# A gated block of mLSTM and differential attention: the queue between mLSTM and branch B, a bank at the start, two loads and two stores

## The chip, the cores and the metric

The kernel runs on one core of one Trainium2 chip. The metric is the device time of one execution in microseconds, smaller being better. The kernel before took 1668.07 us (median of three runs, 1665.59 to 1670.39).

Names of engines: PE is TensorE (matmuls; PEld its weight loads), DVE is VectorE, ACT is ScalarE, POOL is GpSimd, SP is SyncE, which here does nothing but issue DMAs. ACT issues some DMAs too.

## The reference

One layer over a sequence of 1024 rows of width 1024, batch 1, all in fp32:

```python
h = rmsnorm(x, norm_g)
a_q, a_k, a_v, a_o, a_z, a_g, b_q, b_k, b_v, b_z, g_a, g_b = split(h @ w_in)
qk = silu(centred_depthwise_conv(concat(a_q, a_k), ml_conv_w))
hm = rmsnorm(mlstm(mq, mk, mv, forward gates) + mlstm(flipped, backward gates), ml_norm_g)   # 4 heads of 256
y_a = hm * sigmoid(a_o) * silu(a_z)
att = softmax(q0 k0) v - lam * softmax(q1 k1) v        # 8 heads, rope on q and k
y_b = rmsnorm(att, da_subln_g) * (1 - lambda_init) * silu(b_z)
mix = sigmoid(g_a + gb[0]) * (y_a @ w_branch_a) + sigmoid(g_b + gb[1]) * (y_b @ w_branch_b)
out = rmsnorm(x + mix @ w_out, final_g)
```

## The kernel before

**Arithmetic.** Every large product is made of three matmuls: each fp32 operand is split into a rounded high part H and a remainder L, and HH, HL and LH are summed in a PSUM bank. So a weight block of 128 columns is loaded into a tile `raw` (L194, 512 KB), rounded into `wH` by ACT (L231) and its remainder `wL` formed by POOL (L237 in eight pieces or L239 in one). There are two `raw` tiles and three each of `wH` and `wL`.

**Stages, in order of time.** (1) The opening: x is normalised (`norm_a` to `norm_c`, in four steps of ACT, DVE and POOL for each of eight row tiles), transposed on PE into banks `xps[0..7]`, and split into `hH`/`hL`. `xps[6]` is a bank of the pool `pj`, which has two; the others are `T` banks. The first projections (`g0`, `g1`, `g2`) start while the second half of x is still being normalised, each in a `pj` bank. `first_part` (L697) has ACT read each of the eight `xps` once more. (2) The other projections for mLSTM, by a seven-product scheme. (3) Attention, its results `yb` stored to DRAM. (4) mLSTM, four heads in four chunks of 256 rows, woven with units of the gate projections `ga`/`gb` (bank `pj`; their tanh goes through the tile `gt` to DRAM). Its results `ya` are stored by `out` (L1401), two per half head. (5) Branch B: eight tiles of `yb` are loaded (`load_y`, L1486, four buffers `yraw`), split into `sl_yb` by ACT (L1488) and DVE (L1489), and multiplied with eight blocks of `w_branch_b`; the first three blocks go through `first_units` (L1506), which interleaves them over the contraction index k, so that it can begin with one `yb` tile. The five others are `mix_units`. (6) Branch A and the output product.

**What sets the order.** `build` makes one list of units, and `run` (L549) emits them, loading a weight block ahead by a rule (`ahead`): the blocks that the next unit needs, and beyond those one more where `room` allows. Within `keep(...)` the engines named keep the order of emission; the others are ordered by the framework's scheduler. Before the change, `keep` held PE alone from the end of the opening on, so SP's queue was the scheduler's. SP issues in order: an issue whose wait is not met holds all behind it.

The places the change touches: the test `ahead` (L552), `first_part` (L695), the store in `out` (L1401), the start of `ml_units` (L1419), where `x["k"](3)` loads the tile `akf` of chunk 3 (L1213) and `x["gb"](0)` the tile `gb` (L1222, gate values read 128 times over), two lines of the opening (L1731), and the lines of `build` between mLSTM and branch B (L1790 on). `weigh` (L1250, L1251) scales the transposed `akf` into `kwH`, `kwL`, which the `state` products (L148) read; `scores` builds its mask with POOL from `gb` (L1305) and ACT (L1307).

## Time and profile before

| | us |
|---|---|
| median of three runs | 1668.07 |
| lowest, highest | 1665.59, 1670.39 |
| the profiled execution | 1669.31 |
| its span | 1667.0 |
| mean granted TensorE clock in it | 0.996 |

The span runs from the first to the last instruction; 2.3 us of the execution lie around it. A row of the timeline is: start, duration, engine, line, operation, output<-input, size, count, and in brackets the engine's idle time just before, with what is thought to have ended it. A row of the windows is: the stretch, its length, then for PE, PEld, DVE, ACT and POOL the busy time and the number of instructions, then the granted PE clock (1.00 is full), the DMA engines' busy share and GB/s. A row of the waits is: the engine that waited, its tile and line, what ended the wait, total us, times, longest.

### The profile page before, as it was taken

How to read it: one execution, taken by the hardware profiler on the slowest of the kernel's cores; microseconds unless marked ns; L12 is line 12 of the kernel's file. 1: busy time of each engine (PE TensorE's matmuls, PEld its weight loads, DVE VectorE, ACT ScalarE, POOL GpSimd, SP SyncE). 2: the span in 40 equal slices, each digit the busy share in tenths (PEclk: the TensorE clock that was granted, in tenths of full speed). 3: DMA queues.
4: the chain of work that ended last, by engine and by line, in shares of the span. 5: the costliest groups of instructions: out<-in, count | busy, mean ns of one | idle time of the engine just before them, and what ended most of it. 6: DMA issues, size and time to landing. Idle time of an engine off the chain costs nothing. (4 is left out here: it accounts for less than half of the span.)

```text
span 1667.0 us, 25342 instructions
## 1 busy us (share of the span) xinstructions
PE 1629.7 (98%) x9335; PEld 1373.8 (82%) x9335; DVE 1018.8 (61%) x1829; ACT 769.3 (46%) x1547; POOL 654.5 (39%) x707
## 2 busy tenths in 40 slices
PE   7999999999999999999999999999999999999998
PEld 5898778878779888889878888888988987888887
DVE  5733787686754776876777676604666664244533
ACT  6433555555533554544554455524566654132221
POOL 3744676767653552533435253032222221222000
PEclk9999999999999999999999999999999999999999
DMA  5433444344452322213232222139876437452222
GB/s 181 152 126 129 123 134 140 117 136 126 127 151 64 89 58 71 63 40 90 57 82 54 62 58 64 44 95 304 254 222 195 151 108 259 153 167 90 76 99 79
DMA packets 189710, 199.76 MB, mean 120 GB/s; under 512 B 11929, under 2 KB 143346, under 8 KB 189586
## 3 DMA queue, kind: packets, MB, share of 16 engines
q1 hardware_dynamic: 187378, 194.19, 38.5%
q10 hardware_dynamic: 2208, 3.95, 0.6%
q8 instruction: 74, 1.21, 0.3%
q14 instruction: 50, 0.41, 0.1%
HBM read 124.60 MB, written 56.72 MB: 109 GB/s over the span
## 5 line engine op out<-in xcount | busy, mean ns | idle before, releaser
L579 PE MATMUL pj<-hH,wH 128*128 128x512 f32 x640 | 261.9, 409 | 1.8 <-POOL rsy L666 1.0
L579 PE MATMUL pj<-hH,wL 128*128 128x512 f32 x640 | 251.5, 393 | 0.8 <-POOL wL L237 0.8
L579 PE MATMUL pj<-hL,wH 128*128 128x512 f32 x640 | 250.7, 392 | 0.6 <-DVE hL L735 0.6
L1101 DVE TENSOR_REDUCE nm<-S 128x1 f32<-128x1024 f32 x128 | 150.7, 1219 | 109.2 <-PE S L1098 109.2
L239 POOL TENSOR_TENSOR wL<-raw,wH 128x1024 fp32r<-128x1024 f32 x33 | 82.4, 2499 | 175.7 <-ACT wH L231 173.3
L1103 ACT ACTIVATE e<-S,nm 128x1024 f32<-128x1024 f32 x128 | 142.7, 1130 | 7.0 <-DVE nm L1101 7.0
L579 PEld LDWEIGHTS pj<-hH,wL 128*128 128x128 f32 x640 | 120.3, 188 | 28.2 <-POOL wL L237 2.2
L579 PEld LDWEIGHTS pj<-hH,wH 128*128 128x128 f32 x640 | 121.0, 189 | 21.5 <-POOL rsy L666 1.4
L579 PEld LDWEIGHTS pj<-hL,wH 128*128 128x128 f32 x640 | 120.8, 189 | 20.3 <-DVE hL L735 1.4
L1122 ACT CAST pH<-T 128x512 fp32r<-128x512 f32 x128 | 68.9, 589 | 147.7 <-PE T L152 147.7
L1098 PE MATMUL S<-kst,qq 64*128 64x512 f32 x768 | 106.2, 408 | 0.0
L231 ACT CAST wH<-raw 128x1024 fp32r<-128x1024 f32 x47 | 49.4, 1052 | 99.3 <-PE pj L579 70.0
L1109 DVE SCALAR_TENSOR_TENSOR e<-e,r,e 128x1024 f32<-128x1024 f32 x64 | 94.0, 1469 | 1.8
L1098 PEld LDWEIGHTS S<-kst,qq 64*128 64x128 f32 x768 | 67.3, 184 | 29.2 <-issue 9.4
L579 PE MATMUL pj<-sl_yb,wH 128*128 128x512 f32 x288 | 88.6, 389 | 0.0
L376 PE MATMUL T<-TH,wH 128*128 128x512 f32 x256 | 85.8, 394 | 2.3 <-ACT u L383 2.3
L523 DVE SCALAR_TENSOR_TENSOR pj<-cin,cols,pj 128x512 f32<-128x512 f32 x128 | 86.9, 746 | 0.0
L376 PE MATMUL T<-TH,wL 128*128 128x512 f32 x256 | 85.3, 394 | 1.6 <-ACT u L383 1.5
L1123 DVE TENSOR_TENSOR pL<-T,pH 128x512 fp32r<-128x512 f32 x128 | 82.0, 680 | 5.9 <-ACT pH L1122 5.9
L217 POOL TENSOR_TENSOR wL<-raw,wH 128x512 fp32r<-128x512 f32 x32 | 47.0, 1486 | 77.7 <-ACT wH L216 72.3
L152 PEld LDWEIGHTS T<-ident,e 128*128 128x128 f32 x512 | 54.9, 141 | 23.8 <-issue 23.7
L601 PE MATMUL pj<-wH,hH 128*128 128x256 f32 x256 | 74.3, 290 | 0.0
(409 smaller groups left out, 4464.4 us busy)
## 6 DMA issues: line engine op xcount, KB each, us to landing
raw<-in_w_in_dram SPq DMA_DIRECT2D x84, 512.0 KB, 3.9
kst<-hl SPq DMA_DIRECT2D x64, 128.0 KB, 2.4
qq<-hl SPq DMA_DIRECT2D x64, 128.0 KB, 2.4
x<-in_x_dram SPq DMA_DIRECT2D x8, 512.0 KB, 5.3
avH<-tz SPq DMA_DIRECT2D x16, 256.0 KB, 2.0
cak<-y SPq DMA_DIRECT2D x16, 256.0 KB, 2.7
cakH<-cin SPq DMA_DIRECT2D x16, 256.0 KB, 4.6
cakL<-tz SPq DMA_DIRECT2D x16, 256.0 KB, 4.4
```

The costliest lines, as they stand in the source:

```text
L152: self.t.transpose(out, in_, self.ident[0:k, 0:k])
L239: self.p.tensor_tensor(out=wL, in0=raw, in1=wHf, op=ALU.subtract)
L376: self.t.matmul(ps, lhsT=l[:, k, :], rhs=r[:, k, :], start=(first and k == 0 and m == 0), stop=(k == 3 and m == 2), skip_group_check=not f ...
L523: v.scalar_tensor_tensor(out=acc, in0=raw[:, o + x:o + x + 512], scalar=w(x), in1=acc, op0=ALU.mult, op1=ALU.add)
L579: self.t.matmul(ps, lhsT=l[:, k, :], rhs=r, start=(n == 0), stop=(n == 23))
L601: self.t.matmul(ps[:, i, :], lhsT=l, rhs=r[:, k, :], start=(kh == 0 and k == 0 and m == 0), stop=(kh == 1 and k == 3 and m == 2))
L1098: self.t.matmul(ps[:, o], lhsT=qq[r, x, c], rhs=k[r, y, o], start=(m == 0), stop=(m == 2))
L1101: v.tensor_reduce(out=nm, in_=ps, axis=AX.X, op=ALU.max, negate=True)
L1103: a.activation(out=e, in_=ps, func=AF.Exp, bias=nm[:, 0:1], accum_out=Z[:, j, t:t + 1])
L1109: v.scalar_tensor_tensor(out=e0, in0=e, scalar=r[:, 0:1], in1=e0, op0=ALU.mult, op1=ALU.add)
L1122: a.copy(pH[:, :, s], ps)
L1123: v.tensor_tensor(out=pL[:, :, s], in0=ps, in1=pH[:, :, s].bitcast(F32), op=ALU.subtract)
```

## The change

Five edits.

1. From the end of mLSTM to the end of branch B's first group SP keeps the order of emission (`keep(E.PE, E.SP)` ... `keep(E.PE)`), and while `hold` is set no weight block is loaded before its unit asks. `wb(1)` and `wb(2)` are called by hand behind the first four and in front of the second four loads of `yb`.
2. The last two stores of `ya` (last head, second half) are issued by ACT instead of SP.
3. At the start of mLSTM the load of `gb` chunk 0 is issued ahead of that of `akf` chunk 3.
4. In the opening, ACT's second reading of `xps[6]`, the `pj` bank, is done where that of `xps[1]` was, and the latter with the rest.
5. `first_part` makes its tile when it is first needed (as `fp(6)` now comes before `fp(2)`).

```diff
@@ run
-                ahead = lambda k: nxt < need or nxt <= need + (4 if k[0] == "sw" else 1) and room(k)
+                ahead = lambda k: nxt < need or not self.hold and nxt <= need + (4 if k[0] == "sw" else 1) and room(k)
@@ first_part
-        if i == 0:
+        if k not in self.f:
@@ out
-            q.dma_start(out=self.ya[2 * n + i][:, half * 512:(half + 1) * 512], in_=g)
+            (a if n == NH_A - 1 and half == 1 else q).dma_start(out=self.ya[2 * n + i][:, half * 512:(half + 1) * 512], in_=g)
@@ ml_units
-        un += x["k"](3) + x["gb"](0) + x["v"](3) + x["k"](2) + x["v"](2) + x["k"](1) + x["v"](1) + x["HL"](0)
+        un += x["gb"](0) + x["k"](3) + x["v"](3) + x["k"](2) + x["v"](2) + x["k"](1) + x["v"](1) + x["HL"](0)
@@ build, opening
-            w.add(ld(0), sp(0), fp(0), sp(1), g0[0], do(self.transpose_last), *[sp(i) for i in range(2, 8)], ld(1), fp(1), nA(4), nA(5), *g0[1:k])
-            w.add(nB(4), nC(4), nA(6), ld(2), nB(5), nC(5), nA(7), fp(2, 3, 4, 5, 6, 7), nB(6), nC(6), nB(7), nC(7), *g1[:k])
+            w.add(ld(0), sp(0), fp(0), sp(1), g0[0], do(self.transpose_last), *[sp(i) for i in range(2, 8)], ld(1), fp(6), nA(4), nA(5), *g0[1:k])
+            w.add(nB(4), nC(4), nA(6), ld(2), nB(5), nC(5), nA(7), fp(1, 2, 3, 4, 5, 7), nB(6), nC(6), nB(7), nC(7), *g1[:k])
@@ build, mLSTM to branch B
-            w.add(wb(0), *rest[:3])
+            w.add(keep(E.PE, E.SP), do(lambda: setattr(self, "hold", True)), wb(0), *rest[:3])
...
-            w.add(*loads[:4], wb(1), *rest[5:12], *loads[4:], *rest[12:])
+            w.add(*loads[:4], wb(1), *rest[5:12], wb(2), *loads[4:], *rest[12:], do(lambda: setattr(self, "hold", False)))
...
-            w.add(leave("h"), enter("wr", "wr"), *group)
+            w.add(leave("h"), enter("wr", "wr"), *group, keep(E.PE))
```

The order of PE and of DVE is the same in both kernels. What moves is on SP and ACT, and one row of POOL changes its form.

SP at the end of mLSTM, before. `ya6`/`ya7` with `gA_14793`/`gA_14795` are the first halves of the last head, with `gA_14971`/`gA_14973` the second; `raw_15094` and `raw_15240` are the blocks 2 and 3 of `w_branch_b`; `yb0` to `yb3` are the first four tiles of attention's result.

```order
L194 DMA raw_15094<-in_w_branch_b_dram 128x8x128
L1401 DMA ya6_88<-gA_14793 128x512
L1401 DMA ya7_89<-gA_14795 128x512
L194 DMA raw_15240<-in_w_branch_b_dram 128x8x128
L1401 DMA ya6_88<-gA_14971 128x512
L1401 DMA ya7_89<-gA_14973 128x512
L1486 DMA yraw_15138<-yb0_90 128x1024
L1486 DMA yraw_15144<-yb1_91 128x1024
L1486 DMA yraw_15150<-yb2_92 128x1024
L1486 DMA yraw_15156<-yb3_93 128x1024
```

The same place now (`raw_15183` is block 2; blocks 3 and 4 follow behind `yb7`):

```order
L1401 DMA ya6_88<-gA_14793 128x512
L1401 DMA ya7_89<-gA_14795 128x512
L1486 DMA yraw_15128<-yb0_90 128x1024
L1486 DMA yraw_15134<-yb1_91 128x1024
L1486 DMA yraw_15140<-yb2_92 128x1024
L1486 DMA yraw_15146<-yb3_93 128x1024
L194 DMA raw_15183<-in_w_branch_b_dram 128x8x128
L1486 DMA yraw_15187<-yb4_94 128x1024
```

Two weight loads and two stores no longer stand ahead of the four loads of `yb`.

ACT at the same place, now. `gt_15165` and `gt_15223` are the tanh of the last two gate banks, `sl_yb_15130` the first high part that branch B multiplies, `wH_15181` the high part of block 2.

```order
L994 DMA tga6_72<-gt_15080 128x512
L1401 DMA ya6_88<-gA_14971 128x512
L1401 DMA ya7_89<-gA_14973 128x512
L993 ACTIVATE gt_15165<-pj_15086,gbh_213 128x512
L994 DMA tga7_73<-gt_15165 128x512
L1488 CAST sl_yb_15130<-yraw_15128 128x1024
L1488 CAST sl_yb_15136<-yraw_15134 128x1024
L993 ACTIVATE gt_15223<-pj_15168,gbh_213 128x512
L1488 CAST sl_yb_15142<-yraw_15140 128x1024
L994 DMA tga7_73<-gt_15223 128x512
L1488 CAST sl_yb_15148<-yraw_15146 128x1024
L231 CAST wH_15181<-raw_15183 128x1024
```

Before, the cast of block 2 stood between the first two `sl_yb`; it now stands behind the fourth, and the two stores stand ahead of `gt_15165`.

The opening on ACT, and the start of mLSTM on SP, as pieces of the difference. On ACT `T` and `pj` are the banks `xps`, `x_226` and `x_228` the fifth and sixth row tiles:

```order
 L734 ACTIVATE hH_187<-T,g_in 128x512
-L697 ACTIVATE f<-T,g_in 128x512
+L697 ACTIVATE f<-pj,g_in 128x512
 L664 ACTIVATE sq,ssqx<-x_226 128x1024
 L664 ACTIVATE sq,ssqx<-x_228 128x1024
```

ACT's second reading of the `pj` bank moves ahead of the squares of the later row tiles, and a `T` bank takes its old place among the readings behind them. On SP `cak_106` is the key tile of the first head and `gg` the gate rows:

```order
 L1169 DMA yb_97<-zg 128x512 x2
+L1222 DMA gb<-gg 128x2x256
 L1213 DMA akf<-cak_106 128x512
-L1222 DMA gb<-gg 128x2x256
 L1230 DMA vH<-avH_3_129 128x2x256
```

The load of `gb` and that of `akf` have changed places; the rest of the queue stands as it was.

## Prediction

> **What bounds it now.** First the page's busy times, then the waits of the engine with the largest, then the timeline round its longest ones.

> ```profile
> PE 1629.7 (98%) x9335; PEld 1373.8 (82%) x9335; DVE 1018.8 (61%) x1829; ACT 769.3 (46%) x1547; POOL 654.5 (39%) x707
> ```

> PE works in 98 % of a span of 1667.0 us. It does the same matmuls in the same order in both kernels, so all that the change can move is PE's idle time, 1667.0 - 1629.7 = 37.3 us, and the stretches in which PE runs at less than the full clock. The waits of PE name two that lie at places of the change; the other two come below, as rows of the timeline.

> ```profile
> PE T L1506 <- ACT sl_yb L1488: 2.7, 1, 2.7
> PE T L148 <- issue: 1.4, 1, 1.4
> ```

> The windows show the clock there and in two undisturbed stretches.

> ```profile
> 1394.60:1401.00 6.40, 5.94 (x13) 4.36 (x14) 5.73 (x4) 5.05 (x6) 2.42 (x1) 0.50 0.86 296
> 1403.00:1430.88 27.88, 27.88 (x124) 23.09 (x123) 11.68 (x12) 9.47 (x9) 4.28 (x2) 1.00 0.74 270
> 1131.00:1135.00 4.00, 3.99 (x16) 3.58 (x17) 1.31 (x3) 0.73 (x2) 0.00 (x0) 0.57 1.06 397
> 1210.00:1212.00 2.00, 1.47 (x11) 1.26 (x11) 1.00 (x3) 2.00 (x7) 0.00 (x0) 1.00 0.68 244
> ```

> Behind the wait of 2.7 us the granted clock was 0.50 for 6.4 us, and behind that of 1.4 us it was 0.57 over 4 us. Where PE idled 2.00 - 1.47 = 0.53 us in pieces, at 1210, it stayed 1.00. So I read a gap of 1.4 us and more as costing twice: itself, and a stretch at half clock behind it.

> **Edits 1 and 2, the boundary.** SP's queue, then the three instructions it and PE wait for, then PE:

> ```profile
> 1367.05 0.99 SPq L1401 DMA_DIRECT2D ya<-gA  x2
> 1385.35 0.38 SPq L194 DMA_DIRECT2D raw<-in_w_branch_b_dram  x1
> 1385.83 1.01 SPq L1401 DMA_DIRECT2D ya<-gA  x2
> 1386.93 9.22 SPq L1486 DMA_DIRECT2D yraw<-yb  x5
> ```

> ```profile
> 1381.93 3.40 POOL L237 TENSOR_TENSOR wL<-raw,wH 128x128 fp32r<-128x128 f32 x8 [3.61 <-ACT wH L231]
> 1382.67 1.41 DVE L1400 SCALAR_TENSOR_TENSOR gA<-T,mlg,gA 128x512 f32<-128x512 f32 x2 [3.56 <-PE T L152]
> 1393.50 1.04 ACT L1488 CAST sl_yb<-yraw 128x1024 fp32r<-128x1024 f32 x1 [6.28 <-DMA tga<-gt]
> ```

> ```profile
> 1391.54 0.39 PE L579 MATMUL pj<-hH,wL 128*128 128x512 f32 x1
> 1394.60 0.80 PE L1506 MATMUL T<-sl_yb,wH 128*128 128x512 f32 x1 [2.67 <-ACT sl_yb L1488]
> 1395.85 0.79 PE L1506 MATMUL T<-sl_yb,wH 128*128 128x512 f32 x1 [0.46 <-DVE sl_yb L1489]
> 1430.88 0.62 PE L579 MATMUL pj<-sl_yb,wH 128*128 128x512 f32 x2
> ```

> SP issues in order and stood still from 1368 to 1385.35, because the third weight block reuses a `raw` tile which POOL reads until 1381.93 + 3.40 = 1385.33. Behind it come two stores of `ya`, whose data DVE has ready at 1382.67 + 1.41 = 1384.08, and only then `yb0`, at 1386.93. ACT's cast starts 6.6 us later; the row names a DMA of `tga`, but its input `yraw` was on the way since 1386.93, and PE starts 0.06 us behind the cast's end at 1394.54.

> Clean cadence: 27.88 us / 123 weight loads = 0.2267 us a matmul. The 1391.54 matmul lets the next start at 1391.77. The three blocks of the first group are 3 x 8 x 2 x 3 = 144 matmuls, 144 x 0.2267 = 32.64 us, so without a wait the next group would start at 1424.41 and not at 1430.88. That is **6.47 us**: 2.83 of gap and 3.64 of the 0.46 wait and the half clock (6.40 x 0.50 = 3.2).

> Does all of it go? Now `yb0` to `yb3` stand right behind the two stores of 1367.05, so at about 1368; `yb3` and all behind it may start some us later, if a DMA semaphore is still in use by a `tga` store. Durations, from the tile view of the `yb` loads, from the issue of `tga6` at 1374.69, and from three rows at the boundary:

> ```profile
> DMA to landing us min/median/max: 4.4/5.7/7.6
> tga<-gt ACTq DMA_DIRECT2D x1, 256.0 KB, 2.0
> ```

> ```profile
> 1386.53 0.69 ACT L993 ACTIVATE gt<-pj,gbh 128x512 f32<-128x512 f32 x1 [4.14 <-PE pj L579]
> 1394.58 1.23 DVE L1489 TENSOR_TENSOR sl_yb<-yraw,sl_yb 128x1024 fp32r<-128x1024 f32 x1 [10.49 <-ACT sl_yb L1488]
> 1395.62 2.42 POOL L239 TENSOR_TENSOR wL<-raw,wH 128x1024 fp32r<-128x1024 f32 x1 [10.29 <-ACT wH L231]
> ```

> The worst start is 1374.69 + 2.0 = 1376.7, the worst landing 1376.7 + 7.6 = 1384.3. The first cast then waits not for data but for its turn on ACT, behind `gt_15165` (end 1387.22) and its store: 1387.6 to 1388.6, the second to 1389.7; DVE's parts end at 1389.8 and 1391.0. All are ready before 1391.77. **What is late next** is block 2, whose cast now stands behind the fourth `sl_yb`: `gt_15223` waits for the last gate matmul (1391.9), with the two casts and a store it ends near 1395.4, block 2's cast near 1396.4, POOL's part 2.42 later near 1398.9. PE multiplies two blocks with the first tiles before it asks for block 2, at its 37th matmul, 1391.77 + 36 x 0.2267 = 1399.9: about 1 us of margin for H and 1.5 for L. The two stores on ACT occupy it about 1 us (SP's pair took 1.01) between `gt` activations with 4.14 us of idle: nothing. The stores of 1367.05 stay. Bounds of the step: 0 (`yb` still held), and -6.5; below that nothing is idle. I take **-6.5**.

> [...]

> **Edits 4 and 5, the opening.**

> ```profile
> 19.91 0.74 ACT L697 ACTIVATE f<-T,g_in 128x512 f32<-128x512 f32 x1
> 19.93 0.74 DVE L735 SCALAR_TENSOR_TENSOR hL<-pj,g_in,hH 128x512 fp32r<-128x512 f32 x1
> 22.56 0.64 ACT L1002 COPY gt<-pj 128x512 f32<-128x512 f32 x1
> 23.34 0.47 PE L579 MATMUL pj<-hH,wH 128*128 128x512 f32 x1 [1.01 <-POOL rsy L666]
> 28.96 0.70 ACT L697 ACTIVATE f<-pj,g_in 128x512 f32<-128x512 f32 x1
> 29.71 0.50 PE L579 MATMUL pj<-hH,wH 128*128 128x512 f32 x1 [0.65 <-ACT f L697]
> 29.96 0.81 DVE L677 TENSOR_SCALAR x<-x,rsy,rsv 128x1024 f32<-128x1024 f32 x1
> 32.57 1.91 PE L152 MATMUL T<-ident,x 128*128 128x128 f32 x16
> 34.23 0.48 PE L579 MATMUL pj<-hH,wH 128*128 128x512 f32 x1
> ```

> Two groups of matmuls wait for a `pj` bank: at 23.34 for the one that ACT's copy frees at 23.20 (the row names POOL, which frees no bank), and at 29.71 for `xps[6]`, which ACT reads only at 28.96 to 29.66. Read early, it is free at about 21.4, and both waits go: 1.01 + 0.65 = 1.66. But the early reading shares the bank with DVE's row at 19.93 and cannot start before 20.67, 0.76 later than the reading that stood there. What follows on ACT slips by as much, the squares and norms of x among it, so that the last row tile, ready at 29.96 + 0.81 = 30.77, comes at about 31.55. PE now arrives at the transposes at 32.57 - 1.66 = 30.91 and takes 1.66 for sixteen; those of the last tile cannot begin before 31.55. If all wait, they end at 33.21 (gain 1.02); if only the last half, at 32.57 (1.66). I take **-1.2**, nearer the first, with bounds 0 (the slip goes further down the norms) and -1.66.

> **Edit 3, the start of mLSTM.**

> ```profile
> 1117.77 0.42 SPq L1213 DMA_DIRECT2D akf<-cak  x1
> 1118.25 0.45 SPq L1222 DMA_DIRECT2D gb<-gg  x1
> ```

> ```profile
> 1125.91 0.60 PE L152 MATMUL T<-ident,akf 128*128 128x128 f32 x4
> 1126.58 1.25 POOL L1305 TENSOR_SCALAR_AFFINE_SELECT W<-gb 128x128 f32<-128x128 f32 x4 [2.92 <-DMA gb<-gg]
> 1126.90 1.56 ACT L1307 ACTIVATE W<-W,gc_negM 128x128 f32<-128x128 f32 x4 [6.14 <-POOL W L1305]
> 1128.37 0.66 ACT L993 ACTIVATE gA<-pj,gbh 128x512 f32<-128x512 f32 x1
> 1130.01 0.36 PE L148 MATMUL T<-vH,kwH 128*128 128x258 f32 x1 [1.41 <-issue]
> ```

> The gap of 1.41 us at 1130.01 is the end of a chain in ACT's order: `gb` lands at 1126.55, POOL and ACT make the mask until 1128.46, ACT's `gA` and a store follow, then `kwH`, which PE needs. With `gb` ahead, its issue is 1118.25 - 1117.77 = 0.48 earlier and its packets no longer queue behind `akf`'s 256 KB, some 0.65 us at the 397 GB/s of the window above: 1.1 earlier, so the gap becomes 0.3. `akf` pays: it lands by as much later than now, and PE asks for it at 1125.91, which may cost 0.2 to 0.6 there. I take **-1.0** for the gap (bounds +0.6, if `akf` is later than that and the chain gains nothing, and -1.4). The half clock behind it cost at most 4.00 x (1 - 0.57) = 1.72; some of the products there wait for `kwH` and `kwL` anyway, so I take **-1.5** (bounds 0 and -1.72). Queue behind it: everything else on SP stands where it stood.

> **Sum.** 1669.31 - 6.5 - 1.2 - 1.0 - 1.5 = **1659.1** for the profiled execution, which was 1.2 above the median of the runs, 1668.07; the median would give 1657.9. I say 1659.0.

> **Rivals.**
> - *The gap at 1130 or its half clock stays* (`akf` late, or 0.3 to 0.5 us being enough): without -1.5 the sum is 1660.6, without -1.0 too 1661.6. For it: one row of 0.57 is little to know the clock by. Against: 1.00 at 1210. Chance 0.30.
> - *Another wait takes the boundary's place*: block 2, or a `yb` tile, late by a few us. It costs up to the 3.64 of the half clock and as much again in waiting: 1661 to 1667. For it: about 1 us of margin; against: the landing times leave the tiles 10 us. Chance 0.08.
> - *The change doesn't bring the loads forward* (`yb` still held to 1385 by a semaphore of a store): only opening and mLSTM remain, 1669.31 - 3.7 = 1665.6. Against: those stores land in 2.0 us. Chance 0.04.
> - *The slow stretches do not come from the gaps* and stay: 2.83 + 0.46 + 1.2 + 1.0 = 5.5 is left, 1663.8. [...] Against: both stretches begin right behind the two longest waits in question. Chance 0.05.
> - *The half clock moves to another cluster of short waits*, since PE reaches them in another rhythm; PE's other waits of this kind are around 1 us. It costs 3: 1662. Chance 0.04.
> - *Slower than before*: block 2's load is now held in SP's order behind `yb3`. If `yb3`'s wait puts block 2's remainder D us late, PE stalls by D - 1.5 and pays the 3.2 of half clock again. That eats the gain of 10.2 from D = 1.5 + 10.2 - 3.2 = 8.5 us on, and at D = 14 the time is 1674.8. For it: the block is no longer loaded ahead by rule. Against: its cast would have to come at 1405, with `yb3` expected to land 20 us before that. Chance 0.04.

> **How the numbers follow.** The forecast with all terms, 1659.1, has 0.45; the rivals 0.30, 0.08, 0.04, 0.05, 0.04, 0.04. The runs of the kernel before spread over 4.8 us, so 2.4 either way on top. The least sum by the bounds is 1669.31 - 6.5 - 1.66 - 1.4 - 1.72 = 1658.0, less 2.4 and the 1.2 by which the profiled execution lay above the median: 1654. Above, the first rival's 1661.6 plus 2.4 is 1664, and 1665 takes in the clock rival and part of the boundary's: what is left out is about 0.15. About 0.3 %, 5.0 us, is what a measurement of this kernel can tell from no change: faster is below 1663.1. The forecast, the first rival, half of the second and half of the fifth make 0.81; same has the rest of these, the third, the fourth and a little of the last, 0.16; slower 0.03.

> **What the profile of the changed kernel would show.** Right: `yraw` issued at about 1368 behind the first `ya` stores; `sl_yb` cast behind `gt_15165`; no gap at L1506's first matmul, and 1.00 in the 6 us behind it; about 32.6 us from it to the next group; no waits for a `pj` bank at 23.3 and 29.7; at L148 a gap below 0.5 us with clock 1.00 behind it. Wrong: a wait of L1506 for `wH` or `wL` of block 2 some 8 us into the group; a wait of the `akf` transposes near 1125; a window of 0.5 in any place where before it was 1.00; a wait for `x` at the transposes longer than the 0.65 taken here.

## The result, and the profile after

The changed kernel took 1658.62 us (median of four runs, 1657.96 to 1659.14), the kernel before 1667.24 us beside it (1665.59 to 1670.39). The ratio is 0.9946 with a 95% interval of 0.9929 to 0.9963: faster by 8.6 us. The profiled execution took 1657.96 us with a span of 1656.1 us, against 1669.31 and 1667.0. The ratios below leave out one execution, of 4640 us, of the kernel with edit 2 alone.

The page's busy times after, and two rows of PE's waits:

```profile
PE 1624.8 (98%) x9335; PEld 1371.3 (83%) x9335; DVE 1019.7 (62%) x1829; ACT 769.0 (46%) x1547; POOL 654.0 (39%) x700
...
PE T L152 <- DVE x L677: 1.4, 3, 0.8
...
PE T L152 <- DMA akf<-cak: 0.2, 1, 0.2
```

PE's idle time fell from 37.3 to 31.3 us, and its busy time by 4.9 us though it does the same 9335 matmuls: that is the clock, as the rows of windows below show. The lines of L1506, of L148 with "issue" and of the two `pj` banks are gone; two small waits came in their place, 0.76 us of that for `x` and the 0.2 for `akf`.

The boundary after, from the timelines of SP, ACT, DVE, POOL and PE:

```profile
1362.57 0.98 SPq L1401 DMA_DIRECT2D ya<-gA  x2
1363.64 8.91 SPq L1486 DMA_DIRECT2D yraw<-yb  x4
1379.98 0.38 SPq L194 DMA_DIRECT2D raw<-in_w_branch_b_dram  x1
...
1383.15 2.00 ACT L1488 CAST sl_yb<-yraw 128x1024 fp32r<-128x1024 f32 x2 [0.40 <-ACT gt L993]
1389.98 1.05 ACT L231 CAST wH<-raw 128x1024 fp32r<-128x1024 f32 x1
...
1384.23 2.36 DVE L1489 TENSOR_TENSOR sl_yb<-yraw,sl_yb 128x1024 fp32r<-128x1024 f32 x2 [4.62 <-ACT sl_yb L1488]
...
1391.16 2.63 POOL L239 TENSOR_TENSOR wL<-raw,wH 128x1024 fp32r<-128x1024 f32 x1 [11.30 <-ACT wH L231]
...
1387.07 0.39 PE L579 MATMUL pj<-hH,wL 128*128 128x512 f32 x1
1387.30 0.62 PE L1506 MATMUL T<-sl_yb,wH 128*128 128x512 f32 x2
1419.94 0.62 PE L579 MATMUL pj<-sl_yb,wH 128*128 128x512 f32 x2
```

The loads of `yb` stand right behind the first stores of `ya`; the first cast waits for `gt`, not for data; PE goes from the gates into branch B without a gap. From the last gate matmul to the next group it is 1419.94 - 1387.07 = 32.87 us, against 1430.88 - 1391.54 = 39.34 before. The windows of the first group and of the stretch behind the start of mLSTM show the clock:

```profile
1387.30:1419.94 32.64, 32.64 (x145) 27.04 (x144) 16.82 (x15) 13.85 (x14) 6.92 (x3) 1.00 0.80 280
1127.07:1133.97 6.90, 6.77 (x41) 5.75 (x39) 3.00 (x7) 3.44 (x6) 0.99 (x3) 1.00 0.95 295
```

The opening, PE before (two rows) and after (three):

```profile
15.35 0.50 PE L579 MATMUL pj<-hL,wH 128*128 128x512 f32 x1 [0.28 <-DVE hL L735]
...
56.86 0.50 PE L579 MATMUL pj<-hH,wL 128*128 128x512 f32 x1 [0.80 <-POOL wL L237]
```

```profile
15.73 0.50 PE L579 MATMUL pj<-hL,wH 128*128 128x512 f32 x1 [0.29 <-DVE hL L735]
31.96 1.64 PE L152 MATMUL T<-ident,x 128*128 128x128 f32 x13 [0.76 <-DVE x L677]
55.97 0.50 PE L579 MATMUL pj<-hH,wL 128*128 128x512 f32 x1 [0.79 <-POOL wL L237]
```

Between the same two matmuls lie 41.51 us before and 40.24 after. Both bank waits are gone, and the transposes wait 0.76 us for `x`. The start of mLSTM after, SP and PE, and behind it two rows of before:

```profile
1115.97 0.43 SPq L1222 DMA_DIRECT2D gb<-gg  x1
1116.45 0.49 SPq L1213 DMA_DIRECT2D akf<-cak  x1
...
1123.88 0.39 PE L579 MATMUL pj<-hH,wL 128*128 128x512 f32 x1
1124.51 0.66 PE L152 MATMUL T<-ident,akf 128*128 128x128 f32 x4 [0.24 <-DMA akf<-cak]
1127.07 0.28 PE L148 MATMUL T<-vH,kwH 128*128 128x258 f32 x1
1133.97 0.66 PE L152 MATMUL T<-ident,akf 128*128 128x128 f32 x4
```

```profile
1125.68 0.39 PE L579 MATMUL pj<-hH,wL 128*128 128x512 f32 x1
...
1138.65 0.66 PE L152 MATMUL T<-ident,akf 128*128 128x128 f32 x4
```

`gb` goes first, the gap of 1.41 us is gone, and the first `akf` transposes start 1124.51 - 1123.88 = 0.63 us after the matmul ahead of them, where the cadence is 0.23: `akf` comes 0.40 us late. From that matmul to the third `akf` transposes it is 10.09 us, against 12.97 before.

### The profile page after: what moved, and what is told of

Read it like the earlier page. It is cut to its first block, busy times and chain, and to the rows that moved or that the text cites. A ratio compares the mean times of both kernels' runs of the same rounds, so it can differ in the third digit from the quotient of the medians.

```text
span 1656.1 us, 25333 instructions
## 1 busy us (share of the span) xinstructions
PE 1624.8 (98%) x9335; PEld 1371.3 (83%) x9335; DVE 1019.7 (62%) x1829; ACT 769.0 (46%) x1547; POOL 654.0 (39%) x700
## 3 DMA queue, kind: packets, MB, share of 16 engines
q10 hardware_dynamic: 2496, 4.47, 0.7%
q8 instruction: 74, 1.21, 0.3%
## 5 line engine op out<-in xcount | busy, mean ns | idle before, releaser
L579 PE MATMUL pj<-hH,wH 128*128 128x512 f32 x640 | 261.3, 408 | 0.1
L579 PE MATMUL pj<-hH,wL 128*128 128x512 f32 x640 | 251.4, 393 | 0.8 <-POOL wL L237 0.8
L579 PE MATMUL pj<-hL,wH 128*128 128x512 f32 x640 | 250.6, 391 | 0.6 <-DVE hL L735 0.6
L239 POOL TENSOR_TENSOR wL<-raw,wH 128x1024 fp32r<-128x1024 f32 x34 | 85.0, 2501 | 173.4 <-ACT wH L231 171.0
L1103 ACT ACTIVATE e<-S,nm 128x1024 f32<-128x1024 f32 x128 | 142.7, 1130 | 7.0 <-DVE nm L1101 7.0
L579 PEld LDWEIGHTS pj<-hH,wL 128*128 128x128 f32 x640 | 120.1, 188 | 28.0 <-POOL wL L237 2.1
L579 PEld LDWEIGHTS pj<-hL,wH 128*128 128x128 f32 x640 | 120.7, 189 | 20.3 <-DVE hL L735 1.5
L579 PEld LDWEIGHTS pj<-hH,wH 128*128 128x128 f32 x640 | 120.8, 189 | 19.1 <-ACT hH L734 0.5
L231 ACT CAST wH<-raw 128x1024 fp32r<-128x1024 f32 x47 | 49.5, 1053 | 94.4 <-PE pj L579 68.6
L579 PE MATMUL pj<-sl_yb,wH 128*128 128x512 f32 x288 | 88.7, 389 | 0.0
L152 PEld LDWEIGHTS T<-ident,e 128*128 128x128 f32 x512 | 54.9, 141 | 23.8 <-issue 23.7
## 6 DMA issues: line engine op xcount, KB each, us to landing
avH<-tz SPq DMA_DIRECT2D x16, 256.0 KB, 2.0
cak<-y SPq DMA_DIRECT2D x16, 256.0 KB, 2.6
cakH<-cin SPq DMA_DIRECT2D x16, 256.0 KB, 4.6
cakL<-tz SPq DMA_DIRECT2D x16, 256.0 KB, 4.4
```

What stands on the lines that cost most here:

```text
L152: self.t.transpose(out, in_, self.ident[0:k, 0:k])
L239: self.p.tensor_tensor(out=wL, in0=raw, in1=wHf, op=ALU.subtract)
L579: self.t.matmul(ps, lhsT=l[:, k, :], rhs=r, start=(n == 0), stop=(n == 23))
L1103: a.activation(out=e, in_=ps, func=AF.Exp, bias=nm[:, 0:1], accum_out=Z[:, j, t:t + 1])
```

## The experiments

Three lengths of the trace serve as a measure for all: **A**, the opening, between the two matmuls above; **B**, the start of mLSTM, as above; **C**, the boundary, last gate matmul to next group. The slow column has the stretches at a granted clock of 0.50 behind B's and C's gaps, in us.

| kernel | A | B | C | slow behind B, C | median, ratio to before (95%) |
|---|---|---|---|---|---|
| before, first profile | 41.51 | 12.97 | 39.34 | 3.41, 6.83 | |
| before again | 41.50 | 12.55 | 39.30 | 3.41, 6.83 | 1668.25, 1.0002 (0.9993 to 1.0011) |
| edits 1 and 2 | 41.48 | 10.94 | 32.86 | none, none | 1661.22, 0.9963 (0.9950 to 0.9975) |
| edits 4 and 5 | 40.26 | 11.26 | 38.20 | none, 3.41 | 1666.79, 0.9991 (0.9982 to 1.0000) |
| edit 3 | 41.51 | 10.04 | 39.56 | none, 6.83 | 1667.07, 0.9994 (0.9985 to 1.0002) |
| edit 2 alone | 41.49 | 11.04 | 35.80 | none, none | 1664.39, 0.9989 (0.9980 to 0.9998) |
| changed, without edit 2 | 40.25 | 10.53 | 33.03 | none, none | 1658.48, 0.9953 (0.9940 to 0.9965) |
| changed, without hold | 40.24 | 10.22 | 32.87 | none, none | 1658.88, 0.9955 (0.9943 to 0.9968) |
| changed | 40.24 | 10.09 | 32.87 | none, none | 1658.62, 0.9946 (0.9929 to 0.9963) |

The lengths come from one profiled execution each. Each edit shortens its own length and leaves the others, but for the gap at L148, which varies, and the clock: B's slow stretch is missing in three kernels that do not touch it.

**The kernel before, once more.** No edit.

> The kernel before, unchanged, profiled a second time, to see whether the two slow stretches belong to every execution. If the gaps cause them: waits of 2.7 us at L1506 and 1.4 us at L148 again, granted clock near 0.5 behind both, span 1667 within 0.5. If they hang on something that varies from one execution to the next (the phase of a clock window, say): one of them shorter or absent, span 1663.5 to 1666. The runs of before that are on record spread over 4.8 us, those of the changed kernel over 1.2, which the second reading would explain.

Neither reading was clean. The gap at L148 was smaller this time:

```profile
1129.37 0.36 PE L148 MATMUL T<-vH,kwH 128*128 128x258 f32 x1 [0.93 <-issue]
```

Yet the stretch behind it was as long as before. Windows cut at its edges, in the first profile of before and in this one:

```profile
1131.49:1134.90 3.41, 3.40 (x15) 3.20 (x15) 0.85 (x2) 0.63 (x2) 0.00 (x0) 0.50 1.06 401
1394.32:1401.14 6.82, 6.08 (x14) 4.41 (x14) 5.89 (x4) 5.47 (x7) 2.42 (x1) 0.50 0.86 301
```

```profile
1130.99:1134.41 3.42, 3.42 (x14) 3.23 (x15) 0.85 (x2) 0.87 (x2) 0.00 (x0) 0.50 1.05 397
1393.82:1400.65 6.83, 6.37 (x14) 4.75 (x15) 6.16 (x5) 5.34 (x6) 2.42 (x1) 0.50 0.89 315
```

The stretches are 3.41 us or twice that, and their starts lie 1394.32 - 1131.49 = 1393.82 - 1130.99 = 262.83 us apart in both: 77 times 3.4133. So the clock goes by windows of 3.41 us that follow each other without a break, a grid; a window at 0.50 is called slow here. Both profiles have one more stretch at 0.50 behind PE's last product, and it starts on the same grid: in the first, at 1663.97, 1663.97 - 1394.32 = 269.65 us or 79 times 3.4133 later. In 90 timed executions of the kernel before, 11 of this run and 79 taken beside the experiments, the mean clock was 0.999 in 3 (median 1665.2 us), 0.998 in 28 (1666.1), 0.997 in 33 (1667.7) and 0.996 in 26 (1669.2). One slow window costs 3.41 x 0.50 = 1.71 us, or 0.001 of the mean clock, and 0.999 is what the changed kernel shows, whose profile has only the stretch behind the last product. So the spread of the kernel before is mostly the number of slow windows while PE works, none to three.

**Edits 1 and 2 alone.** Two of the changed lines:

```diff
 w.add(wb(0), *rest[:3])   ->   w.add(keep(E.PE, E.SP), do(... "hold", True), wb(0), *rest[:3])
 q.dma_start(out=self.ya[...])   ->   (a if n == NH_A - 1 and half == 1 else q).dma_start(...)
```

> Before plus edits 1 and 2 alone (order kept on SP, no block ahead, last ya stores by ACT). Theory: L1506 starts without a gap, granted clock 1.00 in the 6 us behind it, first group 32.64 us long; the step is -6.5 us in the trace, opening and start of mLSTM as before (gaps 1.0, 0.65 and 1.4). Rival, the slow stretch is not due to the gap: clock 0.50 remains, the step is -3.3. Rival, the gain needs the earlier edits too: the gap stays above 1 us.

C fell by 39.34 - 32.86 = 6.48 us, at full clock. The windows of the first group and behind the gap at L148, and that gap:

```profile
1390.56:1423.20 32.64, 32.64 (x145) 27.03 (x144) 16.81 (x15) 13.85 (x14) 6.91 (x3) 1.00 0.81 280
1130.39:1137.00 6.61, 6.47 (x36) 5.38 (x37) 2.76 (x7) 3.43 (x6) 0.50 (x2) 1.00 0.96 349
...
1130.39 0.36 PE L148 MATMUL T<-vH,kwH 128*128 128x258 f32 x1 [0.91 <-issue]
```

The second row is the surprise: at L148 PE had idled 0.91 us, as long as in the run above, and the clock stayed at 1.00. The length of the gap that a row names does not decide.

**Edits 4 and 5 alone.**

```diff
-... ld(1), fp(1), nA(4) ... fp(2, 3, 4, 5, 6, 7)
+... ld(1), fp(6), nA(4) ... fp(1, 2, 3, 4, 5, 7)
```

> Before plus edits 4 and 5 alone (ACT reads the pj bank early). Theory: the waits at 23.3 and 29.7 vanish, a wait of 0.6 to 0.8 us for x appears at the transposes, and PE stands 0.9 us ahead from 34 us on to the end; boundary and mLSTM as before. A further 0.9 us which the changed kernel gained between 60 and 990 us: if it follows from the opening, it shows here too (1.8 ahead at 986 us); if it differs from execution to execution, not.

A fell by 1.25 us. The further 0.9 us between 57 and 1124 us did not come: over the nine profiles of the table, which are the same there, this stretch was 1067.9 us (the changed kernel) to 1069.4 long, 1068.8 in the first profile of before and 1068.9 here. It varies by execution. At the boundary this run splits one gap over two windows of its grid (PE's column is modelled):

```profile
1387.35:1390.76 3.41, 1.94 (x9) 1.28 (x7) 0.00 (x0) 0.18 (x1) 0.00 (x0) 1.00 1.01 394
1390.76:1394.18 3.42, 1.75 (x6) 1.24 (x7) 1.85 (x2) 3.42 (x5) 1.47 (x1) 1.00 0.85 326
1394.18:1397.59 3.41, 3.41 (x9) 2.67 (x8) 3.41 (x3) 2.03 (x3) 0.96 (x1) 0.50 0.94 309
```

After the first of them the clock stayed, after the second it halved.

**Edit 3 alone.**

```diff
-un += x["k"](3) + x["gb"](0) + ...
+un += x["gb"](0) + x["k"](3) + ...
```

> Before plus edit 3 alone (gb issued ahead of akf). Theory: the gap of 1.41 at L148 goes, akf costs 0.2 to 0.5 us, the clock behind it is 1.00: 2.6 to 3.0 us ahead at 1135. Rival, the half clock has another cause: clock 0.57 remains and only 1.0 to 1.3 us are gained. Boundary as before: 2.7 us wait and 0.50 behind it.

B fell to 10.04: 2.93 less than in the first profile of before, but 0.90 to 1.22 less than in the three profiles with the gap and without a slow window (10.94 to 11.26). The gap, less what `akf` costs, is worth about 1.1; the window is worth 1.7 in those executions that have one. The time fell by only 0.06 % by the ratio, and the interval holds no change.

**The changed kernel without edit 2, edit 2 alone, and the changed kernel without the hold.**

```diff
-(a if n == NH_A - 1 and half == 1 else q).dma_start(...)
+q.dma_start(...)
```

> The changed kernel with edit 2 undone: the two last stores of ya on SP again, in order of emission ahead of the loads of yb. Theory: SP now waits for DVE's L1400 (ends 1379.6 in the changed kernel), then 1.0 us for the stores; yb0 goes at about 1380.7 instead of 1363.6, lands 5.2 to 6.6 later, and the first cast ends at 1387.0 to 1388.4 where PE wants it at 1387.3: a gap of 0 to 1.1 at L1506 and 0.5 to 1.2 more for DVE's part; the time is 0.5 to 2.3 us above that of the changed kernel, plus 1.7 in executions where a clock window is hit. Rival, the stores' place does not matter since the transfers share the same engines: 0.

The reverse edit on the kernel before:

> Before plus edit 2 alone (the two stores by ACT, SP's order left to the scheduler). Theory: SP still stands at block 3 until POOL has read its raw tile (1385.33 in before), so yb0 goes at 1385.8 instead of 1386.9: the gap of 2.7 becomes 1.6, the time falls by 1.1, and by 1.7 or 3.4 more in executions where fewer clock windows are hit. Rival, the stores were what held the loads: the gap goes and 6.5 us are gained.

```diff
-do(lambda: setattr(self, "hold", True))
+do(lambda: setattr(self, "hold", False))
```

> The changed kernel without the hold: SP keeps the order of emission, but block 2 may be loaded ahead by rule, and then stands ahead of the first halves of ya and of yb0. Theory: its raw tile is free at 1362.1 (POOL's end in the changed kernel), before the stores' data are ready at 1363, so nothing is held for long; yb0 goes within 1 us of 1363.6, no gap at L1506, time as the changed kernel within 0.5 us. Rival, the hold is what keeps the loads early: a gap above 1 us comes back.

With the stores on SP, `yb0` goes 17 us later, and next to nothing is lost, C being 33.03 (SP, ACT and PE of that run):

```profile
1381.13 1.87 SPq L1486 DMA_DIRECT2D yraw<-yb  x4
...
1384.94 1.05 ACT L1488 CAST sl_yb<-yraw 128x1024 fp32r<-128x1024 f32 x1 [1.11 <-DMA yraw<-yb]
...
1388.38 0.61 PE L1506 MATMUL T<-sl_yb,wH 128*128 128x512 f32 x2
```

The load is there after 3.8 us, not the 5.2 to 6.6 that I had expected, and the cast ends at 1385.99, 2.4 us before PE asks for it. So the expectation of 0.5 to 2.3 us was too high, and the rival's number came: the stores' place does not matter here. The run does not show the reason that the rival gives; in the profile of before a 256 KB store by ACT was there 2.0 us after its issue at 1374.69, where SP issued nothing, and one at 1387.25, among the loads of `yb`, 6.6 us after its issue. With edit 2 alone the loads still stand behind block 3 (SP and PE):

```profile
1383.77 0.38 SPq L194 DMA_DIRECT2D raw<-in_w_branch_b_dram  x1
1384.24 2.05 SPq L1486 DMA_DIRECT2D yraw<-yb  x4
...
1390.88 0.50 PE L1506 MATMUL T<-sl_yb,wH 128*128 128x512 f32 x1 [0.53 <-ACT sl_yb L1488]
1392.13 0.50 PE L1506 MATMUL T<-sl_yb,wH 128*128 128x512 f32 x1 [0.76 <-DVE sl_yb L1489]
```

The gap of 2.67 became 0.53 rather than 1.6, since the first cast starts at 1389.77, 5.5 us behind the issue of its load, where it was 6.6 in before; and C is 3.5 below before: the shorter gap and no slow window, against two waits of 0.76 and 0.74 us for DVE where before had one of 0.46. The time fell by only 0.11 % by the ratio. Without the hold, block 2's load stands ahead of the stores and waits for nothing:

```profile
1362.33 0.38 SPq L194 DMA_DIRECT2D raw<-in_w_branch_b_dram  x1
1362.83 0.99 SPq L1401 DMA_DIRECT2D ya<-gA  x2
1363.91 23.29 SPq L1486 DMA_DIRECT2D yraw<-yb  x6
```

`yb0` goes at 1363.91, and C is 32.87. What does the work is SP's order of emission, which puts block 3 behind the loads; the hold and the stores on ACT, each left out alone, are not needed for the time. No run leaves out both, and none keeps SP's order without the calls of `wb(1)` and `wb(2)` by hand.

**Gaps of a chosen length.** DVE forms the remainder of a `yb` tile several times over, to the same result, so that PE waits for it; nothing else is added.

```diff
-self.v.tensor_tensor(out=l, in0=raw, in1=h.bitcast(F32), op=ALU.subtract)
+[self.v.tensor_tensor(...) for _ in range({0: 5}.get(i, 1) if src is self.yb else 1)]
```

> The changed kernel with DVE forming the remainder of the first yb tile five times over (the same result), so that PE's second matmul of branch B waits for it: one gap of about 2.5 us at the boundary. The slow stretches of the traces so far are 3.41 or 6.83 us long, and within an execution their starts lie a whole multiple of 3.413 us apart. Theory: the clock is set by windows of 3.41 us on a grid that does not follow the program, and halves for a window when PE was active for less than about half of the window before. A gap of 2.5 us leaves one window below half in some three quarters of the executions: the profile shows 0.50 for 3.41 or 6.83 us, the time is above that of the changed kernel by 2.6 in some runs and by 4.3 or 6.0 in most, and mean clocks spread over 0.997 to 0.999. Rival, the slow stretches do not come from gaps of this size: +2.6, clock 0.999 in all runs.

The two-gap run has `{0: 4, 2: 5}`.

> As the run with one gap, but four times over for the first yb tile and five times for the third: two gaps of about 1.4 and 1.6 us some 5.5 us apart, 3.0 us of idle time in all. Theory (share of a window): each gap leaves every window above half, so no slow stretch; +3.0, clock 0.999 in nearly all runs, and a median below that of the run with one gap although PE idles longer. Rival (length of a gap from about 1.4 us on, as I read the profile of before): half clock behind each, +6 or more.

Both misfired: the scheduler spread the repetitions among the other tiles, and PE waited 8.82 us in the one, 4.39 and 2.81 in the other (1670.17 and 1669.38 us). They bear on the grid all the same. In the first run 10.24 us were at 0.50, three windows, from 1392.65 on, inside the gap, to 5.3 us behind it; in the two-gap run one window lay behind each gap:

```profile
1392.73:1396.15 3.42, 3.42 (x9) 2.65 (x10) 3.42 (x2) 0.74 (x1) 2.07 (x1) 0.50 0.52 157
...
1402.97:1406.39 3.42, 3.42 (x9) 2.67 (x9) 2.08 (x2) 0.94 (x1) 0.00 (x0) 0.50 0.99 374
```

They begin 1402.97 - 1392.73 = 10.24 us apart: three times 3.413. With DVE's order kept as well (`keep(E.PE, E.SP, E.DVE)`):

> The run with one gap again, with DVE's order kept too, since in that run the scheduler had spread the repetitions among the later tiles and the gap came out at 8.8 us. Five times over for the first tile in a row: DVE ends at about 1390.2 on the changed kernel's clock, PE's second matmul waits from 1387.5: one gap of 2.5 us. Theory (a window of 3.41 us in which PE was active for less than about half is followed by one at half clock): in some three quarters of the executions 3.41 or 6.83 us at 0.50, so 2.5, 4.2 or 5.9 us above the changed kernel, mean clocks of 0.997 to 0.999. [...]

> The run with two gaps again, with DVE's order kept: four times over for the first tile, five for the third: gaps of about 1.4 and 1.7 us, 7 us apart. Theory (share of a window): both leave every window above or near half, so slow windows in few executions: +3.1 us over the changed kernel, at most 4.8, though the idle time is 0.6 longer than in the run with one gap. Rival (any gap from 1.4 us on): 3.41 us at 0.50 behind each, +6.5.

One gap of 2.86 us (the wait, and the windows before and at the slow stretch):

```profile
1391.61 0.50 PE L1506 MATMUL T<-sl_yb,wH 128*128 128x512 f32 x1 [2.86 <-DVE sl_yb L1489]
...
1389.10:1392.51 3.41, 0.90 (x4) 0.76 (x5) 3.38 (x3) 3.01 (x4) 1.69 (x1) 1.00 0.20 77
1392.51:1395.92 3.41, 3.41 (x10) 2.63 (x9) 3.41 (x2) 0.08 (x1) 1.29 (x1) 0.50 0.52 163
```

The six runs gave 1661.99 us at mean clock 0.999 and 1662.83 to 1663.71 at 0.998: five of six, by the mean clock, with one slow window. The median, 1663.21, is 4.6 above the changed kernel; in the profile C is 37.64, or 4.8 longer, of which the window is 1.7 and the gap 3.1. So a gap of 2.86 us, shorter than one window of the grid, had a slow window behind it. The two-gap run missed its forecast of 3.1 to 4.8: its median is 1666.29, 7.7 above the changed kernel. The second gap came out at 3.62 us, since one of DVE's subtractions for the third tile took 3.30 us where the median is 1.22; the first, 1.60 us, lies whole in one window of the grid:

```profile
1387.14:1390.55 3.41, 1.81 (x8) 1.20 (x7) 3.38 (x4) 2.60 (x4) 0.00 (x0) 1.00 0.33 97
1390.55:1393.96 3.41, 3.41 (x16) 2.80 (x16) 3.38 (x2) 1.30 (x3) 3.04 (x1) 1.00 0.83 280
...
1397.38:1404.20 6.82, 5.47 (x13) 4.33 (x14) 5.63 (x6) 1.04 (x1) 0.00 (x0) 0.50 0.61 184
```

Behind the first gap the clock is 1.00; only the second is followed by 0.50. A gap longer than the 1.41 us of before thus cost nothing beyond itself. (Neither of the two runs with this design gave two short gaps; the comparison of one long gap with two short ones of the same sum stays unmade.)

## Why the prediction was right, and where its reasons were not

The forecast was 1659.0 us in 1654 to 1665; 1658.62 came. By its own steps:

**The boundary, -6.5: measured -6.47** (39.34 to 32.87). The chain ran as worked out: PE was 4.47 us ahead when it came there, so the first cast, expected at 1387.6, was due at 1383.1 (1383.15), block 2's cast at 1391.9 (1389.98 to 1391.03) and POOL's part at 1394.4 (1391.16 + 2.63 = 1393.79). PE asked for block 2 at 1387.30 + 8.16 = 1395.46, so the margin was 1.7 us, and the rivals that block 2 would be late fell. (Two slips in that step: what it calls the third weight block is block 3, the fourth; and its "about 1 us of margin for H" does not follow from its own times, 1399.9 - 1396.4 = 3.5. In the trace it was 4.4.) What the step did not separate, the runs did: of edits 1 and 2, SP's order carries the gain, and the stores by ACT add nothing to it (1658.48 us without them, 1658.62 with).

**The opening, -1.2: measured -1.27** (41.51 to 40.24), and -1.25 with the two edits alone; the wait for `x` that takes the place is 0.76 us where 0.65 was expected. ACT's early reading of the `pj` bank came behind DVE's, as reckoned: in the changed kernel it starts at 21.09, after a wait of 0.64 us for DVE's, which ends at 20.31 + 0.75 = 21.06.

**The start of mLSTM, -1.0 and -1.5: measured -2.88** (12.97 to 10.09) against the first profile of before. The gap's part, with `akf` 0.40 us late (0.2 to 0.6 were expected), is 0.9 to 1.2. The half clock was put a little low: a full window of 1.71 went.

**The step that failed is the reading of the clock**: "a gap of 1.4 us and more as costing twice". A gap of 0.93 us was followed by a slow window, gaps of 0.91, 1.01 (edit 2 alone), 1.21 (edits 4 and 5) and 1.60 were not. What the rows fit is a grid of 3.413 us, fixed within an execution, and the work that PE does in each window of it. The modelled PE column is too coarse to show this. Here are the window ahead of the slow one in the repeat of before, and the window with the gap of 0.91 us in the run of edits 1 and 2:

```profile
1127.58:1130.99 3.41, 2.34 (x10) 1.29 (x9) 0.97 (x2) 1.51 (x3) 0.00 (x0) 1.00 1.08 390
1127.96:1131.37 3.41, 2.38 (x10) 1.41 (x8) 0.50 (x2) 2.07 (x5) 0.00 (x0) 1.00 1.08 390
```

They look alike, and only the first was followed by 0.50. Both hold products of 258 columns, which the trace models at 0.28 to 0.39 us though they follow each other every 0.12 us at full clock. So count each product by its spacing at full clock (medians of the profile of before: 0.227 us for 512 columns, 0.12 for 256 and 258, 0.109 for a transpose of 128), and the same at half clock. Then the two windows hold 1.39 and 1.69 us of work. Counted like this over the grids of all thirteen profiles, from 57 us to PE's last product, every window with 1.39 us of work or less was followed by half clock, and every window with 1.52 or more was not; none lies between. A limit of 0.41 to 0.45 of a window (1.39 and 1.52 of 3.41 us) is thus an estimate worked out from these traces, not a measured one; the "less than about half" of the expectations was the author's estimate ahead of the count. It covers the way back too: a slow window in which PE had no wait holds 1.57 to 1.71 us of such work, one with a wait held 1.18 at most.

The rival that the slow stretches do not come from the gaps falls: where edits 1 and 2 took the 2.67 us at the boundary away, the 6.83 us at 0.50 went with them, and a gap of 2.86 us put there brought 3.41 us back.

**Why the profile gained more than the medians.** Lengths A, B and C give -1.27 - 2.88 - 6.47 = -10.6, and the span fell by 10.9, while the medians differ by 8.6, or by 8.9 against the 90 executions (1667.5). The sum was made against an execution with three slow windows, the median one of before has two: 1.7 us of the -10.2 was there to be gained only in a part of the executions. Two more differences between the two profiled executions are chance: the changed kernel's ran 0.9 us shorter between 57 and 1124 us, and started 0.4 us later. So the nearness of the number is in part luck. For the median the sum gave 1657.9, and the text says 1659.0 without a reason; with one window less to gain, the 90 executions give 1667.5 - 8.5 = 1659.0. The changed kernel spreads over 1.2 us where the kernel before spreads over 4.8; the slow windows are what it lost.

## What to carry to other kernels

When a queue that issues in order stands still for a tile, look at what else is queued behind that issue: here one weight load (block 3, waiting until 1385.35 and first multiplied at 1430.88) held the four loads that the next stage began with. Move the waiting issue back; who issues the rest mattered little. In this kernel a gap on TensorE cost itself, and by where the grid fell nothing more (0.91 and 1.60 us) or half of one to three 3.41 us windows (0.93, 2.67 and 8.82 us); count such windows (0.50 in the rows of windows, 0.001 of this kernel's mean clock each) in several executions before sizing a change by one profile.
